# Two factors of a state-space input table turned once, kept in DRAM and multiplied per batch on VectorE

## The chip, the cores and the metric

One core of a Trainium2 chip runs the whole kernel; the other cores are idle. The metric is the device time of one execution in microseconds (us). The engines have these names in the profile: PE (TensorE, matmuls; PEld is its weight load), DVE (VectorE), ACT (ScalarE), POOL (GpSimd) and SP (SyncE, which here issues all the transfers, in its own order).

## The reference, cut to what matters

Two layers work on x of 1024 frames by 1024 channels. Layer 0 projects RMSNorm(x) into a state-space branch, a retention branch and their gates; layer 1 is a convolution module. The change concerns the state-space branch: 64 groups of 16 channels, each group with 64 complex states.

```python
dt  = exp(log_dt)
lb  = exp((a_re + 1j * a_im) * dt)              # one complex factor per group and state
bb  = (lb - 1) / a * (b_re + 1j * b_im)         # group x state x channel of the group
bu  = einsum('tgh,gnh->tgn', u, bb)             # input, 16 channels -> 64 states
x_t = lb * x_(t-1) + bu_t                       # scan over the frames
y   = Re(einsum('tgn,ghn->tgh', x, c)) + d * u
y   = gelu(y); y = y * sigmoid(y @ glu_w + glu_b)
y   = y * silu(gate)
```

The real and imaginary parts are float32 arrays of their own.

## The kernel before, in words

**Numbers.** The large matmuls split each float32 operand into a high and a low part and add three products (`mm3`, lines 137 to 144), all in one accumulation: 24 matmuls of 128x512 for one output tile of 128 channels by 512 frames. An output block `u0` to `u7` (state-space input) or `g8` to `g23` (gates) has two such tiles, 48 matmuls. A weight block is loaded from DRAM (`wload_pieces`, line 131), rounded to its high part on ACT (line 133), and the low part is formed by DVE or POOL (line 134); for the gate blocks that is DVE. Three buffers of each allow loads two blocks ahead. The matmul results go to three PSUM banks in turn (`mm`); DVE evicts a gate tile (line 325), ACT applies SiLU (line 326), SP stores it (line 329).

**The state-space branch in frames of 8.** The scan runs over blocks of 8 frames, so a state is carried 128 times, not 1024. For that each group needs tables: `M`, the input table (powers of `lb` for the 8 frames times `bb`); `Tc` and `Ts`, rotations that make the scan real; `W3`, the output table. `s5_params` forms the small factors for all groups on DVE and POOL: `pr`, `pi` (nine powers by 32 pairs of groups) and `bbr`, `bbi` (32 pairs by 16 channels), each with 128 partitions: two groups by 64 states.

**Batches.** The 64 groups are worked in 8 batches `B` of 8 groups (four pairs `q`). For each batch:
- `s5_tables(B)` has POOL form `M`, then `Tc` and `Ts`, then `W3`: 18 operations of 128x512 in a fixed chain over all batches. `Mr` and `Mi` have one buffer each; so the table of the next batch is written after `kp` of this batch has read it.
- `s5_states(B)`: SP loads the inputs `U` (line 678). PE turns `Mr` and `Mi` by four transposes each into PSUM (line 685) and ACT copies them to SBUF (line 687): this is `W2`, with 8 frames by 16 channels on the partitions and the states along the row. PE multiplies `W2` with `U` into `v` (line 696, 32 matmuls of 128 columns). DVE rotates (`m0`, `m1`), scans (line 711), rotates back (`d0`, `d1`) and writes the states `S`, of which there is one buffer (lines 704 to 724). PE forms the kernel of the short convolution, `kp`, from `Mr` and `Mi` (lines 730, 731) and turns it (`kt`, line 736); ACT copies it (`Kt`); SP stores it to DRAM (line 740) and loads it back skewed (`Wd`, line 743); ACT copies it to `W1` (line 745).
- `s5_out(B)`: PE forms `y` from `W1`, `U`, `W3`, `S` (lines 760, 766), ACT copies it (`yb`, line 770), SP stores it (line 772).

**Order of the work.** `layer0_front` runs two gate blocks per batch (lines 347 to 355): states of batch B, gate block, outputs of batch B - 1, gate block, tables of batch B + 1. A scheduler that plans with priorities in program order decides the final order on each engine; an engine then works strictly in that order and waits on semaphores. The gate matmuls fill PE between the small state-space products. The temporaries of the scan (`m0`, `m1`, `d0`, `d1`) share the four buffers of the tag `tmpV`; those of POOL have two of `tmpP`. The small products use five PSUM banks (`aux`).

After this stage come retention, the GLU and the output projection, and layer 1.

Of the kernel before, what the change touches and what calls it, by code (L numbers as in the profile page):

```python
# [11 lines left out]
F32 = mybir.dt.float32  # L12
# [3 lines left out]
ALU = mybir.AluOpType  # L16
# [3 lines left out]
P = 128  # L20
# [19 lines left out]
class Trunk:  # L40
# [163 lines left out]
    def layer0_front(self, st):  # L204
        tc, nc, A = self.tc, self.nc, self.A
# [30 lines left out]
        for kb in range(KB):  # L236
# [6 lines left out]
            t = xt[kb] = ev.tile([P, T], F32, name=f"x_{kb}", tag="xin", bufs=8)  # L243
            g = self.vec(V_NG0, kb)
            for h in range(2):
                c = slice(h * HALF, (h + 1) * HALF)
# [50 lines left out]
        def scaled(nb, w, name, cb):  # L297
            for h in range(2):
                ps = self.bank(f"mm_{name}_{h}", aux=False)
                self.gemm(ps[:], w, xs[h], {2: r_mm[h]} if nb == 2 else None)  # L300
                cb(h, ps)
# [18 lines left out]
        def gate_block(nb, w, dst):  # L320
            gt = uv.tile([P, T], F32, name=f"gt_{nb}", tag="ut", bufs=2)

            def evac(h, ps):
                c = slice(h * HALF, (h + 1) * HALF)
                nc.vector.tensor_tensor(gt[:, c], ps[:], self.R[:, c], op=ALU.mult)  # L325
                nc.scalar.activation(gt[:, c], gt[:, c], AF.Silu)
            scaled(nb, w, f"g{nb}", evac)
            k = nb % 8
            nc.sync.dma_start(dst[k * P:(k + 1) * P], gt[:])
# [17 lines left out]
        for nb in range(8, 24):  # L347
            B = (nb - 8) // 2
            if nb % 2 == 0:
                self.s5_states(B)  # L350
            gate_block(nb, self.wnext(f"g{nb}"), self.gs_d if nb < 16 else self.gr_d)
            if nb % 2 == 0 and B:
                self.s5_out(B - 1)
            if nb % 2 and B < 7:
                self.s5_tables(B + 1)
# [277 lines left out]
    def outer(self, B, o_r, o_i, ar, ai, br, bi, view, op_r=ALU.subtract, op_i=ALU.add):  # L633

        gp = self.nc.gpsimd
        for o, op, (a0, b0), (a1, b1) in ((o_r, op_r, (ar, br), (ai, bi)), (o_i, op_i, (ar, bi), (ai, br))):
# [2 lines left out]
            yield gp.tensor_tensor(view(o), a0, b0, op=ALU.mult)  # L639
            yield gp.tensor_tensor(o, o, t[:], op=op)  # L640

    def s5_tables(self, B):


        nc, w = self.nc, self.s5
        gp, v = nc.gpsimd, nc.vector
        qs = slice(4 * B, 4 * B + 4)

        Mr, Mi = self.big(f"Mr_{B}", "Mr", 1), self.big(f"Mi_{B}", "Mi", 1)
        vm = lambda ap: ap.rearrange("p q (j h) -> p q j h", j=8)  # L650
        bj = lambda t: t[:, qs, :].unsqueeze(2).broadcast_to([P, 4, 8, 16])
        pj = lambda t, o=0: t[:, o:o + 8, qs].rearrange("p j q -> p q j").unsqueeze(3).broadcast_to([P, 4, 8, 16])
        made = [self.outer(B, Mr[:], Mi[:], bj(self.bbr), bj(self.bbi), pj(self.pr), pj(self.pi), vm)]

        Tc, Ts = self.big(f"Tc_{B}", "Tc", 2), self.big(f"Ts_{B}", "Ts", 2)
        vt = lambda ap: ap.rearrange("p q (a b) -> p q a b", b=16)
        ea = lambda t: t[:, 0:8, qs].rearrange("p a q -> p q a").unsqueeze(3).broadcast_to([P, 4, 8, 16])
        eb = lambda t: t[:, 0:16, qs].rearrange("p b q -> p q b").unsqueeze(2).broadcast_to([P, 4, 8, 16])
        made.append(self.outer(B, Tc[:], Ts[:], ea(self.e2[0]), ea(self.e2[1]), eb(self.e1[0]), eb(self.e1[1]), vt))

        W3 = w.tile([P, 2, 4, P], F32, name=f"W3_{B}", tag="W3", bufs=2)
        made.append(self.outer(B, W3[:, 0], W3[:, 1], pj(self.pr, 1), pj(self.pi, 1), bj(self.cr), bj(self.nci), vm,
                               ALU.add, ALU.subtract))
        self.s5_last = self.chained(chain(*made), self.s5_last)
        R8 = self.big(f"R8_{B}", "R8", 2)
        for q in range(4):
            nc.scalar.mul(R8[:, q, :], self.m01[:], self.r8[:, 4 * B + q:4 * B + q + 1])
        self.s5_tab[B] = Mr, Mi, W3, Tc, Ts, R8

    def s5_states(self, B):  # L670
        nc, w = self.nc, self.s5
        gp, v = nc.gpsimd, nc.vector
        q0 = 4 * B
        Mr, Mi, W3, Tc, Ts, R8 = self.s5_tab.pop(B)


        U = w.tile([P, 8, P], F32, name=f"U_{B}", tag="U", bufs=2)
        nc.sync.dma_start(U[:], self.u_d[B].rearrange("j h g m -> (j h) g m"))


        W2 = []
        for nm, M in (("r", Mr), ("i", Mi)):
            ps = self.bank(f"w2{nm}_{B}")
            for q in range(4):
                nc.tensor.transpose(ps[:, q * P:(q + 1) * P], M[:, q, :], self.ident[:])
            t = self.big(f"W2{nm}_{B}", f"W2{nm}", 1)
            nc.scalar.copy(t[:].rearrange("p q n -> p (q n)"), ps[:])
            W2.append(t)

        V = []  # L690
        for c in range(2):
            ps = self.bank(f"v{c}_{B}")
            for q in range(4):
                for g2 in range(2):
                    r = slice(64 * g2, 64 * g2 + 64)
                    nc.tensor.matmul(ps[r, q * P:(q + 1) * P], W2[c][:, q, r], U[:, 2 * q + g2, :],
                                     start=True, stop=True)
            V.append(ps)
        fl = lambda t: t[:].rearrange("p q n -> p (q n)")

        tc, ts = fl(Tc), fl(Ts)
        vr, vi = V[0][:], V[1][:]
        t2, t4 = (fl(self.big(f"m{i}_{B}", "tmpV", 4)) for i in range(2))
        v.tensor_tensor(t2, vi, ts, op=ALU.mult)
        v.tensor_tensor(t4, vr, ts, op=ALU.mult)
        v.tensor_tensor(vr, vr, tc, op=ALU.mult)
        v.tensor_tensor(vi, vi, tc, op=ALU.mult)
        v.tensor_tensor(vr, vr, t2, op=ALU.add)
        v.tensor_tensor(vi, vi, t4, op=ALU.subtract)
        for z in (vr, vi):  # L710
            v.tensor_tensor_scan(z, fl(R8), z, 0.0, op0=ALU.mult, op1=ALU.add)

        S = w.tile([P, 2, 4, P], F32, name=f"S_{B}", tag="S", bufs=1)
        c1 = lambda t: t[:, :, 1:P]
        c0 = lambda t: t[:, :, 0:P - 1]
        zr, zi = (z.rearrange("p (q n) -> p q n", q=4) for z in (vr, vi))
        t2, t3 = (self.big(f"d{i}_{B}", "tmpV", 4) for i in range(2))
        v.tensor_tensor(c0(t2), c0(zi), c0(Ts), op=ALU.mult)
        v.tensor_tensor(c0(t3), c0(zr), c0(Ts), op=ALU.mult)
        v.tensor_tensor(c0(zr), c0(zr), c0(Tc), op=ALU.mult)  # L720
        v.tensor_tensor(c0(zi), c0(zi), c0(Tc), op=ALU.mult)
        v.tensor_tensor(c1(S[:, 0]), c0(zr), c0(t2), op=ALU.subtract)
        v.tensor_tensor(c1(S[:, 1]), c0(zi), c0(t3), op=ALU.add)
        v.memset(S[:].rearrange("p c q m -> p (c q) m")[:, :, 0:1], 0.0)


        kp = self.bank(f"kp_{B}")
        for q in range(4):
            o = kp[q * 32:(q + 1) * 32, :P]
            nc.tensor.matmul(o, self.cbr[:, q0 + q, :], Mr[:, q, :], start=True, stop=False)  # L730
            nc.tensor.matmul(o, self.cbni[:, q0 + q, :], Mi[:, q, :], start=False, stop=True)
        Kg = w.tile([P, P], F32, name=f"Kg_{B}", tag="Kg", bufs=1)
        nc.scalar.copy(Kg[:], kp[:, :P])
        v.tensor_tensor(Kg[:, :16], Kg[:, :16], self.dd[:, B, :], op=ALU.add)
        kp = self.bank(f"kt_{B}")
        nc.tensor.transpose(kp[:, :P], Kg[:], self.ident[:])
        Kt = w.tile([P, P], F32, name=f"Kt_{B}", tag="Kg", bufs=1)
        nc.scalar.copy(Kt[:], kp[:, :P])

        nc.sync.dma_start(self.k_d[B, 112:], Kt[:])  # L740
        Wd = w.tile([P, 8, P], F32, name=f"Wd_{B}", tag="yb", bufs=1)
        kd = self.k_d[B]
        nc.sync.dma_start(Wd[:], bass.AP(tensor=kd.tensor, offset=kd.offset, ap=[[P, P], [16 * P, 8], [1, P]]))
        W1 = w.tile([P, 8, P], F32, name=f"W1_{B}", tag="W1", bufs=2)
        nc.scalar.copy(W1[:].rearrange("p g (i h) -> p i g h", i=8), Wd[:].rearrange("p i (g h) -> p i g h", g=8))
        self.s5_back[B] = U, W1, W3, S
# [693 lines left out]
```

## Time and profile before

| what | value |
|---|---|
| time, median of 3 runs | 1219.36 us (1218.27 to 1221.7) |
| time of the profiled execution | 1219.24 us |
| its span, first to last instruction | 1217.5 us |
| mean granted clock of PE | 0.997 |
| `u` and start of the stage, first transposes of batch 0 | 101.20 us |
| `v` of batches 1 to 7 | 132.69, 162.21, 191.72, 221.23, 250.75, 280.26, 309.77 us |
| last `y` of the stage | 335.17 to 337.15 us |
| DVE, POOL busy in 150 to 200 us | 24.68 of 50, 38.61 of 50 us |
| DMA share in 100 to 300 us, per 50 us | 0.31, 0.35, 0.42, 0.35 |

How to read it: the span is cut by engine, line and tile names; a busy time is that of the instructions on one engine. The chain of waits follows the program back from its last instruction, at each step to what released it. Where an engine isn't on that chain, its idle time costs nothing by itself.

### The profile page before, as it was taken

To read this page: it belongs to the slowest core of one execution; us is meant where nothing else is said; L and a number is where in the kernel's file an instruction comes from. 1 tells how busy PE (TensorE), PEld (TensorE's weight loads), DVE (VectorE), ACT (ScalarE), POOL (GpSimd) and SP (SyncE) were. 2 spreads that over 40 slices of the span, in tenths; PEclk is the share of its full clock that TensorE was granted. 3 is DMA by queue.
4 is the path that set the end of the run, shared out by engine and by line. 5 is a ranking of instruction groups with operands and counts; after the bars stand their busy time and mean duration, and the time that the engine had idled before them with its cause. 6 is when DMAs were issued, how large, how long until landed. Compare 5 with 4: busy or idle time off the path is not lost.

```text
span 1217.5 us, 17581 instructions
## 1 busy us (share of the span) xinstructions
PE 1199.5 (99%) x6660; PEld 1011.3 (83%) x6660; DVE 747.1 (61%) x1337; ACT 480.6 (39%) x712; POOL 653.9 (54%) x453
## 2 busy tenths in 40 slices
PE   9999999999999999998999999999999999999997
PEld 7888888888889999997888888788888888888876
DVE  7965555555413635546746101599999799999533
ACT  7212233322222323134434322545545575434652
POOL 2059988888124333342454551578453467758642
PEclk9999999999999999999999999999999999999998
DMA  8342433333384536266446776755677654356764
GB/s 333 104 139 74 152 128 124 133 131 124 107 268 139 176 102 195 82 216 220 165 156 216 269 270 254 260 188 196 222 253 251 232 182 155 123 176 236 243 250 147
DMA packets 98500, 225.03 MB, mean 185 GB/s; under 512 B 9072, under 2 KB 38000, under 8 KB 97776
## 3 DMA queue, kind: packets, MB, share of 16 engines
q1 hardware_dynamic: 98416, 223.92, 54.9%
q8 instruction: 52, 0.85, 0.3%
q14 instruction: 32, 0.26, 0.1%
HBM read 158.41 MB, written 61.28 MB: 180 GB/s over the span
## 4 chain that ended last, share of the span: by engine, by line
PE 91%; DMA 4%; DVE 2%; ACT 1%; POOL 1%; issue 1%; SPq 1%; DVEq 0%; POOLq 0%
PE mm_g L143 7%; PE mm_g L144 7%; PE mm_g L142 7%; PE mm_wo L144 5%; PE mm_wo L142 5%; PE mm_wo L143 5%; PE mm_a L144 2%; PE mm_b L144 2%; PE mm_a L143 2%; PE mm_a L142 2%; PE mm_b L143 2%; PE mm_u L144 2%; PE mm_u L143 2%; PE mm_b L142 2%; PE mm_u L142 2%; PE mm_glu L144 2%
## 5 line engine op out<-in xcount | busy, mean ns | idle before, releaser
L1142 DVE SCALAR_TENSOR_TENSOR cv<-u,convw,cv 128x512 f32<-128x512 f32 x398 | 273.4, 751 | 11.9 <-ACT cv L1128 9.6
L1122 POOL TENSOR_TENSOR tp<-tp,tp 128x512 f32<-128x512 f32 x64 | 83.1, 1298 | 44.4 <-ACT tp L1121 43.3
L144 PE MATMUL mm_g<-xh,wl_g 128*128 128x512 f32 x256 | 100.8, 394 | 0.0
L143 PE MATMUL mm_g<-xl,wh_g 128*128 128x512 f32 x256 | 100.6, 393 | 0.0
L142 PE MATMUL mm_g<-xh,wh_g 128*128 128x512 f32 x256 | 100.5, 393 | 0.0
L861 PE MATMUL mm_v<-wh_v,xl 128*128 128x256 f32 x256 | 72.5, 283 | 0.0
L860 PE MATMUL mm_v<-wl_v,xh 128*128 128x256 f32 x256 | 72.4, 283 | 0.0
L859 PE MATMUL mm_v<-wh_v,xh 128*128 128x256 f32 x256 | 72.4, 283 | 0.0
L134 POOL TENSOR_TENSOR wl_v<-wf_v,wh_v 128x1024 fp32r<-128x1024 f32 x8 | 19.2, 2396 | 88.6 <-ACT wh_v L133 88.6
L1121 ACT ACTIVATE tp<-u,convw 128x512 f32<-128x512 f32 x64 | 45.7, 719 | 34.9 <-POOL tp L1122 33.2
L325 DVE TENSOR_TENSOR gt<-mm_g,R 128x512 f32<-128x512 f32 x32 | 21.9, 685 | 59.9 <-PE mm_g L144 59.9
L143 PEld LDWEIGHTS mm_g<-xl,wh_g 128*128 128x128 f32 x256 | 48.1, 188 | 11.3 <-issue 1.6
L144 PEld LDWEIGHTS mm_g<-xh,wl_g 128*128 128x128 f32 x256 | 48.0, 188 | 10.6
L142 PEld LDWEIGHTS mm_g<-xh,wh_g 128*128 128x128 f32 x256 | 48.1, 188 | 9.6
L144 PE MATMUL mm_oc<-zh,wl_woc 128*128 128x512 f32 (+1 forms) x152 | 54.0, 359 | 1.5 <-DMA wl_woc<-lo_woc 1.5
L1044 DVE TENSOR_TENSOR x<-mm_wo,xr 128x512 f32<-128x512 f32 x16 | 11.1, 692 | 71.9 <-PE mm_wo L144 51.4
L142 PE MATMUL mm_oc<-zh,wh_woc 128*128 128x512 f32 (+1 forms) x152 | 54.3, 363 | 0.0
L143 PE MATMUL mm_oc<-zl,wh_woc 128*128 128x512 f32 (+1 forms) x152 | 53.8, 357 | 0.5 <-POOL zl L969 0.5
L143 PE MATMUL mm_glu<-yl,wh_glu 128*128 128x512 f32 x128 | 50.3, 393 | 2.5 <-DVE yl L969 2.5
L144 PE MATMUL mm_wo<-yrh,wl_wor 128*128 128x512 f32 x128 | 50.0, 391 | 1.4 <-DMA wl_wor<-lo_wor 1.4
L143 PE MATMUL mm_u<-xl,wh_u 128*128 128x512 f32 x128 | 50.1, 391 | 0.8 <-DVE xl L257 0.7
L142 PE MATMUL mm_glu<-yh,wh_glu 128*128 128x512 f32 x128 | 50.1, 393 | 0.6 <-ACT yh L968 0.6
(393 smaller groups left out, 3600.7 us busy)
## 6 DMA issues: line engine op xcount, KB each, us to landing
wf_g<-w_ab SPq DMA_DIRECT2D x16, 512.0 KB, 4.0
wf_wos<-w_out SPq DMA_DIRECT2D x16, 512.0 KB, 5.0
wf_wor<-w_out SPq DMA_DIRECT2D x16, 512.0 KB, 5.8
wf_cb<-w_c SPq DMA_DIRECT2D x16, 512.0 KB, 4.4
wf_ca<-w_c SPq DMA_DIRECT2D x16, 512.0 KB, 4.7
wf_woc<-w_out_c SPq DMA_DIRECT2D x16, 512.0 KB, 5.0
wf_cg<-w_c SPq DMA_DIRECT2D x11, 512.0 KB, 4.4
u_d<-ut SPq DMA_DIRECT2D x8, 512.0 KB, 3.2
```

Source lines behind the costliest of these rows:

```text
L134: lo[i].tensor_tensor(wl[:].rearrange(fl)[:, c], wf[:, c], h.bitcast(F32), op=ALU.subtract)
L142: nc.tensor.matmul(ps, wh[:, kb, :], xh, start=start, stop=False)
L143: nc.tensor.matmul(ps, wh[:, kb, :], xl, start=False, stop=False)
L144: self.last_mm = nc.tensor.matmul(ps, wl[:, kb, :], xh, start=False, stop=stop)
L325: nc.vector.tensor_tensor(gt[:, c], ps[:], self.R[:, c], op=ALU.mult)
L859: nc.tensor.matmul(ps[:, :256], xh[:, o:o + P], wh, start=kb == 0, stop=False)
L860: nc.tensor.matmul(ps[:, :256], xh[:, o:o + P], wl, start=False, stop=False)
L861: nc.tensor.matmul(ps[:, :256], xl[:, o:o + P], wh, start=False, stop=kb == KB - 1)
L1044: v.tensor_tensor(t[:], ps[:], xt[:], op=ALU.add)
L1121: nc.scalar.mul(sk[:], u[:, k:k + HALF], cw[:, nb, k:k + 1])
L1122: gp.tensor_tensor(s0[:], s0[:], sk[:], op=ALU.add)
L1142: v.scalar_tensor_tensor(dst[:], *tap, accs_[i][:], op0=ALU.mult, op1=ALU.add)
```

## The change

After the states of batch 0, `s5_turned` is called once. It copies `bbr` and `bbi` into an order by channel (ACT), turns them and the first eight powers `pr`, `pi` with twelve transposes on PE, copies the three results to SBUF (ACT), and stores them to two DRAM tensors: `pt_d` (a row for each frame of 8 and pair of groups, 128 states long) and `bt_d` (a row for each of 16 channels and pair).

For each batch from 1 on, `s5_tables` now ends with `s5_w2(B)`. SP loads four tables of 128x512: `PTr` and `PTi` repeat a row of powers for the 16 channels, `BTr` and `BTi` repeat a row of `bb` for the 8 frames, so that partition (frame, channel) has both factors beside each other. Six DVE operations multiply them as complex numbers into `W2r` and `W2i`. The states of that batch use these; the transposes of line 685 and the copies of line 687 are left for batch 0 alone. POOL still forms `M` for all batches, since `kp` reads it.

The four loaded tables, the two reordered copies and the three turned ones all use the tag `tmpV`, with its four buffers as before. The order of the loads on the SP queue and of the six products on DVE is the scheduler's. In the built program it is, for batches 4 to 7 on SP: `PTr`, `BTr`, `k_d` of the batch before, `Wd`, a gate store, `U` (before or behind the gate store), a weight block, `PTi`, the store of `yb`, `BTi`. For batches 2 and 3 `BTi` is issued ahead of the store of `yb`. On DVE the first product (`W2r`) stands behind the rotations of the batch before, the other five behind its `S`, with the gate evictions between them.

```diff
@@ layer0_front
             if nb % 2 == 0:
                 self.s5_states(B)
+                if B == 0:
+                    self.s5_turned()
@@
+    def s5_turned(self):
+        nc = self.nc
+        self.pt_d = self.dram.tile([2, 2, P, P], F32, name="pt_d")
+        self.bt_d = self.dram.tile([2, 4, P, P], F32, name="bt_d")
+        fl = lambda t, a, n: t[:, a * n:(a + 1) * n, :].rearrange("p a b -> p (a b)")
+        order = [self.big(f"hq{c}", "tmpV", 4) for c in range(2)]
+        for o, t in zip(order, (self.bbr, self.bbi)):
+            nc.scalar.copy(o[:].rearrange("p a (h q) -> p (a h) q", h=4), t[:].rearrange("p q h -> p h q"))
+        for i, (dst, parts) in enumerate((
+                (self.pt_d[:].rearrange("c a r n -> r (c a) n"), [fl(t, a, 4) for t in (self.pr, self.pi) for a in range(2)]),
+                (self.bt_d[0].rearrange("a r n -> r a n"), [order[0][:, a, :] for a in range(4)]),
+                (self.bt_d[1].rearrange("a r n -> r a n"), [order[1][:, a, :] for a in range(4)]))):
+            ps = self.bank(f"turn{i}")
+            for a, src in enumerate(parts):
+                nc.tensor.transpose(ps[:, a * P:(a + 1) * P], src, self.ident[:])
+            t = self.big(f"turned{i}", "tmpV", 4)
+            nc.scalar.copy(t[:].rearrange("p q n -> p (q n)"), ps[:])
+            nc.sync.dma_start(dst, t[:])
+
+    def s5_w2(self, B):
+        nc, v = self.nc, self.nc.vector
+        (ptr, pti), (btr, bti) = ([self.big(f"{n}{c}_{B}", "tmpV", 4) for c in "ri"] for n in ("PT", "BT"))
+        dp, db = self.pt_d, self.bt_d
+        for c, (pt, bt) in enumerate(((ptr, btr), (pti, bti))):
+            nc.sync.dma_start(pt[:].rearrange("p q n -> p (q n)"),
+                              bass.AP(tensor=dp.tensor, offset=dp.offset + (c * 2 * P + 4 * B) * P,
+                                      ap=[[32 * P, 8], [0, 16], [1, 4 * P]]))
+            nc.sync.dma_start(bt[:].rearrange("p q n -> p (q n)"), bass.AP(tensor=db.tensor, offset=db.offset + (c * 4 * P + 4 * B) * P,
+                                                ap=[[0, 8], [32 * P, 16], [1, 4 * P]]))
+        w2r, w2i = (self.big(f"W2{nm}_{B}", f"W2{nm}", 1) for nm in "ri")
+        v.tensor_tensor(w2r[:], ptr[:], btr[:], op=ALU.mult)
+        v.tensor_tensor(w2i[:], ptr[:], bti[:], op=ALU.mult)
+        v.tensor_tensor(ptr[:], pti[:], bti[:], op=ALU.mult)
+        v.tensor_tensor(pti[:], pti[:], btr[:], op=ALU.mult)
+        v.tensor_tensor(w2r[:], w2r[:], ptr[:], op=ALU.subtract)
+        v.tensor_tensor(w2i[:], w2i[:], pti[:], op=ALU.add)
+        return [w2r, w2i]
@@ s5_tables
-        self.s5_tab[B] = Mr, Mi, W3, Tc, Ts, R8
+        self.s5_tab[B] = Mr, Mi, W3, Tc, Ts, R8, self.s5_w2(B) if B else None
@@ s5_states
-        Mr, Mi, W3, Tc, Ts, R8 = self.s5_tab.pop(B)
+        Mr, Mi, W3, Tc, Ts, R8, W2 = self.s5_tab.pop(B)
...
-        W2 = []
-        for nm, M in (("r", Mr), ("i", Mi)):
+        first, W2 = W2 is None, W2 or []
+        for nm, M in (("r", Mr), ("i", Mi)) if first else ():
             ps = self.bank(f"w2{nm}_{B}")
```

## The prediction

> **What bounds the kernel now.** I read the page's busy table and slices first, then the waits of TensorE (PE), then the chain of waits over the state-space stage (about 101 to 337 us), and last the timelines of the other engines there.
>
> ```profile
> PE 1199.5 (99%) x6660; PEld 1011.3 (83%) x6660; DVE 747.1 (61%) x1337; ACT 480.6 (39%) x712; POOL 653.9 (54%) x453
> ...
> POOL 2059988888124333342454551578453467758642
> PEclk9999999999999999999999999999999999999998
> ```
>
> PE is busy for 99% of the span at full granted clock; POOL (GpSimd) is nearly full in slices 4 to 10, the stage of this change. The waits of PE over the whole span begin with 2.5 us for `yl`, and none belongs to the state-space products. The chain in order of time shows the stage as a stretch of PE work alone (start, length, what):
>
> ```profile
> 244.84 0.44 PE w2r L685 x4
> 245.27 0.44 PE w2i L685 x4
> ...
> 250.75 1.90 PE v L696 x32
> ```
>
> So here every microsecond of PE work taken out shortens the kernel, and every wait put on PE lengthens it. One batch of eight takes 29.51 us (`v` at 221.23 and at 250.75), in which PE does 96 gate matmuls, one each 0.227 us.
>
> **What is removed and added on PE.** Batches 1 to 7 lose eight transposes: 0.44 + 0.43 us on the path, 0.87 each, 6.1 us in all. The one-time turn adds twelve of the same form, 12 x 0.109 = 1.3 us. Net -4.8 us, if PE never waits. The fourteen ACT copies that go (0.58 us each) and the five that come are off the path: ACT is 39% busy.
>
> **What is added on DVE (VectorE).** Six products per batch, each 128x512 float32 with both inputs in SBUF. The trace has that form: `yl` alone takes 0.68. Beside a busy POOL it doesn't (first row DVE, then POOL; then the same again):
>
> ```profile
> 366.07 2.88 DVE L836 TENSOR_TENSOR krot<-kraw,kswp 128x512 f32<-128x512 f32 x1 [1.20 <-POOL kswp L835]
> ...
> 366.00 2.40 POOL L134 TENSOR_TENSOR wl_k<-wf_k,wh_k 128x1024 fp32r<-128x1024 f32 x1
> ...
> 548.17 3.48 DVE L969 TENSOR_TENSOR yl<-yf,yh 128x512 fp32r<-128x512 f32 x2
> ...
> 549.37 1.74 POOL L1016 TENSOR_TENSOR yg<-yg,yn 128x512 f32<-128x512 f32 x1
> ```
>
> `krot` ends only 0.5 us after the POOL operation beside it. Two `yl` in a row take 3.48, 1.74 each, and POOL's own 1.29 becomes 1.74: the two engines take turns, a whole operation at a time. In the stage POOL issues table operations of 1.1 to 1.4 us back to back, so I price a product at 0.68 (free) to 1.74 (in turns), near 1.7 while POOL is busy, 0.6 for one that starts on an idle POOL.
> [...]
>
> Six times 1.7 is 10 us per batch on an engine with some 14 free of 29.5, so DVE doesn't become the bound; the question is when the last product is ready. `v` of the next batch must wait for it, and behind `v` on PE lies everything else. POOL's operations stretch by 0.45 per product, some 2.7 us per batch, of the 4 to 5 us that it idles for `kp`: no cost.
>
> **What sets the time of the last product.** The four loads per batch go into the four `tmpV` buffers that the scan of the batch before (`m0`, `m1`, `d0`, `d1`) holds; two wait until `S` is formed. In the built program's order on the SP queue, for batches 4 to 7, the last (`BTi`) is also behind the store of `yb`, which waits for the copies of `yb`, which on ACT come after the copy of `W1`, which waits for the load of `Wd`. Before, that chain read:
>
> ```profile
> 262.36 0.32 SPq L740 DMA_DIRECT2D k_d<-Kt  x1
> ...
> 263.92 0.37 SPq L743 DMA_DIRECT2D Wd<-k_d  x1
> ...
> 271.74 0.32 SPq L772 DMA_DIRECT2D y_d<-yb  x1
> ...
> 269.56 1.05 ACT L745 COPY W<-Wd 128x1024 f32<-128x1024 f32 x1 [5.86 <-DMA Wd<-k_d]
> 270.64 1.07 ACT L770 COPY yb<-y 128x512 f32<-128x512 f32 x2
> ```
>
> The store is issued 21.0 us after `v` (250.75). The new order puts the copy of `Kt` ahead of a weight cast (1.03), so I take 20.2. `BTi` follows at 20.6. It is 256 KB in rows of 2 KB, like these:
>
> ```profile
> yg<-gs_d SPq DMA_DIRECT2D x16, 256.0 KB, 3.2
> yn<-yn_d SPq DMA_DIRECT2D x16, 256.0 KB, 2.8
> ```
>
> With the store's 512 KB just ahead (2.6 us) I take 3.8: landed at 24.4. No row shows sixteen partitions reading one DRAM row; the bounds are 2.8 and the 8.4 us of `s_s_br` (256 KB behind a full queue).
>
> From 24.4 DVE does a product (25.5), the gate's eviction (26.1), and the next two in turns with POOL (27.2, 28.9). POOL started 2.6 after `v`, has 24.2 us of work (223.85 to 248.08) and four stretches, so it ends near 28.6; the subtraction then ends at 29.5 if POOL has finished, 30.6 if not: 30.05. Unhindered, PE reaches the next `v` after 94 matmuls here, 94 x 0.227 + 2.49 (`v`, `kp`) + 3.78 (`y`) + 0.11 = 27.7, or 96 and 28.2. So a batch waits 2.4 or 1.9 us. What queues behind: on SP the gate's store and the next weight load (20 us early); on DVE the next gate evictions, with three PSUM banks of 5.45 us each as cover.
>
> By the same steps:
> - Batch 1: turn, store to DRAM, load back. `turned2` waits on ACT behind two gate copies; store about 125, last load lands about 132, last product about 139, against `v` at 138.1 (126.78 + 44 x 0.227 + 1.3): 1.0 us, 0 to 3.
> - Batch 2: its `v` comes only 77 matmuls after batch 1's, 23.85 us; `BTr` lands at 14.6, so `S` and `BTi` are late (20.2), and the products meet a full POOL: 26.4, and the second part another 1.1 late. 3.7 us, 1.5 to 5.
> - Batch 3: `BTi` goes ahead of the store of `yb`: lands at 19, ready 25.1 against 25.2; the second part 0.7 late.
> - Batch 4: 2.4. Batches 5 and 6: 1.9 each. Batch 7: 0.5, since `Kt` needn't wait for the copies of `R8` (1.3).
>
> Together 12.1 us of new waits.
>
> **The sum.** -6.1 + 1.3 + 12.1 = +7.3. The profiled execution took 1219.24 (span 1217.5 and 1.7 around it), 0.1 below the median shown, 1219.36; the forecast is 1226.5. One microsecond either way in the landing of `BTi` moves five batches, 5 us, and the turns on POOL two or three more: its own range is 1220 to 1235.
>
> [...]
>
> **Rivals.**
> - *The products are ready in time.* If loads land in 2.8 us and products cost 0.68, batch 5 has `BTi` at 23.4 and the subtraction at 26.5, before 28.2; batch 2, with BTi at 19.8, at 22.9, before 23.85. Then only -4.8 is left: 1214.4. For it: `yl` at 0.68 and DVE's free time. Against it: 1.74 beside POOL.
> - *Waits and savings cancel.* Landings 1.0 us earlier and POOL done sooner: waits of 4 to 6 us: 1219.
> - *The loads are the slow part (slower, far).* Many partitions read one DRAM row, with 1 MB more per batch in a stage that moves 100 to 150 GB/s. From a landing over 5 us this decides: at 8.4, 4.6 later, six batches lose 28 us more: 1254. For it: `Wd`, an overlapping read too, takes 5.2 for 512 KB. Against it: that isn't above its like; the DMA share is 0.31 to 0.42.
> - *DVE becomes the bound of the stage (slower).* 15 us of DVE work now (24.7 to 29.3 per 50 us) and 10 of products stay under 28.6 us per batch. It decides from a product of 2.3 us on; at `krot`'s 2.88 a batch takes 15 + 17.3 = 32.3, so 2.8 more than 29.51, times 7, plus 1.3: 1240. Against it: no operation of POOL in the stage is as long as the 2.40 beside `krot`, but when DVE stretches it.
>
> **How the numbers follow.** Forecast (1220 to 1235) 0.55, in time 0.15, cancel 0.15, slow loads 0.07, DVE bound 0.08. 0.3% is 3.7 us, about what a measurement of this kernel can tell from no change. Below 1215.7: the first rival, 0.15. Within: the second, and the lower edge of the forecast, 0.20 together. Above 1223: 0.65. The range 1214 to 1240 leaves out half of the first rival and of the bound by DVE, and the slow loads: 0.19.
>
> **What would show it.** PE's waits: `v` for the last subtraction or addition, 0.5 to 4 us in most batches; the period of `v` near 30 us for batches 4 to 6 rather than 28.6. DVE: products of 1.2 to 1.8 while POOL is busy, 0.68 after. SP: `BTi` issued right behind the store of `yb`, landing in 3 to 5 us. `w2r` and `w2i` four transposes each, batch 0 alone. I am wrong if PE waits for nothing in the stage, if the loads take 2.5 or 8 us, or if the wait ends on POOL or a weight load.

## The result, and the profile after

The changed kernel takes 1235.47 us (median of 6 runs, 1232.12 to 1238.74) against 1219.26 of the kernel before in the same series: a ratio of 1.013, 95% interval 1.0112 to 1.0147, or some 16 us more. The profiled execution took 1235.18 us, its span is 1233.4. Line numbers of the changed kernel are higher by 43 behind the new functions: `v` is L739, the products are L677 to L682, the loads L671 (`PT`) and L674 (`BT`).

The page of the changed kernel, its busy table and slices:

```profile
PE 1201.5 (97%) x6616; PEld 1012.3 (82%) x6616; DVE 788.3 (64%) x1379; ACT 478.0 (39%) x703; POOL 652.1 (53%) x453
...
PE   9999888999999999999999999999999999999997
...
POOL 2069577787414152433354552388463368767642
PEclk9999889999999999999999999999999999999999
```

PE lost 44 instructions, as the change says, and yet is busy 2.0 us longer. The eighths stand in slices 5 to 7 (123 to 216 us), in PE's own row and in two slices of the granted clock: all that was lost lies in the state-space stage. POOL is no longer full there. PE's waits in the stage (line, what it waited for: us in all, times, longest):

```profile
PE v L739 <- issue: 7.5, 2, 4.2
PE v L739 <- DVE W2r L681: 3.7, 1, 3.7
PE v L739 <- ACT wh_g L133: 1.7, 2, 0.9
PE v L739 <- DVE W2i L682: 1.7, 1, 1.7
PE v L739 <- ACT wh_k L133: 0.5, 1, 0.5
```

There were none before; now there are 15.2 us, every one on `v`. "issue" stands where the profile shows nothing that the engine waited for. Where "issue" or ACT's cast `wh_g` is named, the cast had long been done, and DVE's subtraction for `W2r` had ended just ahead of `v`.

The chain in order of time (start, length, what), from the turn to the `v` of batch 2:

```profile
121.49 4.46 DMA pt_d<-turned
...
127.33 5.72 DMA bt_d<-turned
133.06 5.57 DMA BTi<-bt_d
138.66 0.70 DVE W2i L678
...
141.46 3.68 PE v L739 x32
...
168.29 4.24 issue
172.52 3.65 PE v L739 x31
```

Where there was only PE before, there is now a store, a load, products, and a `v` that takes 3.68 us where it took 1.90. The windows around the first wait say why (stretch, its length, then busy time with instructions of PE, PEld, DVE, ACT, POOL, then the granted clock, DMA share and GB/s):

```profile
137.80:139.60 1.80, 0.00 (x1) 0.00 (x0) 0.91 (x2) 0.00 (x0) 0.00 (x0) 1.00 0.81 245
139.70:141.40 1.70, 0.00 (x0) 0.00 (x0) 1.67 (x4) 0.00 (x0) 0.00 (x0) 0.58 0.48 195
141.40:146.80 5.40, 5.34 (x50) 4.54 (x51) 2.77 (x6) 0.89 (x2) 0.51 (x1) 0.50 0.00 1
146.80:150.00 3.20, 3.20 (x16) 2.61 (x15) 3.20 (x6) 1.60 (x2) 3.12 (x4) 1.00 0.02 5
```

The granted clock falls to 0.50 within the second stretch, some 2 us into the wait, and stays there through the third, for 5.3 us of PE's work.

The SP queue ahead of the last load for batch 5, and DVE behind it:

```profile
246.81 0.38 SPq L786 DMA_DIRECT2D Wd<-k_d  x1
249.16 0.32 SPq L329 DMA_DIRECT2D gr_d<-gt  x1
249.53 0.42 SPq L721 DMA_DIRECT2D U<-u_d  x1
250.23 0.49 SPq L131 DMA_DIRECT2D wf_g<-w_ab  x1
250.82 0.60 SPq L671 DMA_DIRECT2D PTi<-pt_d  x1
252.24 0.31 SPq L815 DMA_DIRECT2D y_d<-yb  x1
252.65 0.60 SPq L674 DMA_DIRECT2D BTi<-bt_d  x1
```

```profile
259.61 0.80 DVE L678 TENSOR_TENSOR W2i<-PTr,BTi 128x512 f32<-128x512 f32 x1 [8.20 <-DMA BTi<-bt_d]
...
261.96 0.69 DVE L680 TENSOR_TENSOR PTi<-PTi,BTr 128x512 f32<-128x512 f32 x1
262.57 0.68 DVE L681 TENSOR_TENSOR W2r<-W2r,PTr 128x512 f32<-128x512 f32 x1
```

`BTi` is issued 18.1 us after `v` (234.54) and is 6.96 us on its way, with 2.75 MB issued in the six microseconds ahead of it; DVE stands idle for it for 8.2 us. The last products then run at 0.68 to 0.69. One of these waits has another cause: the 1.7 us before the second half of batch 7's `v` come from the last addition, which stood beside a POOL operation of 2.45 us (`wl_k`, line 134):

```profile
322.00 2.84 DVE L682 TENSOR_TENSOR W2i<-W2i,PTi 128x512 f32<-128x512 f32 x1
```

From the start of the first `v` to the end of the last `y`, the stage went from 230.1 to 247.6 us. PE's work there at full clock is 230.1 - 6.1 + 1.3 = 225.3; its waits are 15.2, and it was busy 232.4, so 7.1 more than its work: that is the lowered clock. What lies ahead of the stage and behind it took 1.6 us less (0.33 and 1.24). The sum is +15.9 of span.

### The profile page after: what moved, and what is told of

Read it like the earlier page. It is cut to its first block, busy times and chain, and to the rows that moved or that the text cites. A ratio compares the mean times of both kernels' runs of the same rounds, so it can differ in the third digit from the quotient of the medians.

```text
span 1233.4 us, 17582 instructions
## 1 busy us (share of the span) xinstructions
PE 1201.5 (97%) x6616; PEld 1012.3 (82%) x6616; DVE 788.3 (64%) x1379; ACT 478.0 (39%) x703; POOL 652.1 (53%) x453
## 4 chain that ended last, share of the span: by engine, by line
PE 82%; DMA 7%; DVE 5%; issue 3%; ACT 2%; POOL 1%; SPq 1%; DVEq 0%; POOLq 0%
PE mm_g L144 5%; PE mm_g L143 5%; PE mm_g L142 5%; PE mm_wo L144 5%; PE mm_wo L143 5%; PE mm_wo L142 5%; PE mm_b L143 2%; PE mm_b L144 2%; PE mm_a L143 2%; PE mm_a L144 2%; PE mm_b L142 2%; PE mm_a L142 2%; PE mm_u L144 2%; PE mm_u L143 2%; PE mm_u L142 2%
## 5 line engine op out<-in xcount | busy, mean ns | idle before, releaser
L326 ACT ACTIVATE gt<-gt 128x512 f32<-128x512 f32 x32 | 20.2, 632 | 112.8 <-DVE gt L325 100.8
```

## The experiments

All are compared with the kernel before on the same chip (its medians there: 1219.3 to 1220.6). Stage: from the first `v` to the end of the last `y` in the profiled run. Clock: PE's busy time there less its work at full clock (230.1 and what was removed and added). Waits: the rest of the stage. Behind: the span from there on, whose work is the same in all.

| kernel | median, us | ratio, 95% | stage | clock | waits | behind |
|---|---|---|---|---|---|---|
| before | 1219.26 | 1 | 230.1 | 0.0 | 0.0 | 880.3 |
| changed | 1235.47 | 1.0112 to 1.0147 | 247.6 | 7.1 | 15.2 | 879.1 |
| e1 own buffers | 1232.16 | 1.0072 to 1.0104 | 242.1 | 4.1 | 12.7 | 881.1 |
| e2 own, from batch 2 | 1221.24 | 0.9986 to 1.0009 | 233.3 | 2.4 | 4.7 | 879.1 |
| e3 turn alone | 1220.97 | 0.9995 to 1.0014 | 231.5 | 0.1 | 0.0 | 881.2 |
| e4 rows apart | 1223.94 | 1.0011 to 1.0038 | 233.2 | 2.2 | 5.8 | 879.0 |
| e5 rows apart, same tensor | 1227.35 | 1.0038 to 1.0088 | 237.4 | 2.4 | 9.7 | 879.4 |
| e6 from batch 4 | 1231.50 | 1.0071 to 1.0111 | 238.4 | 3.7 | 6.8 | 883.9 |
| e7 28 transposes | 1234.95 | 1.0103 to 1.0145 | 247.8 | 3.4 | 9.4 | 878.3 |
| e8 own, from batch 3 | 1224.09 | 1.0017 to 1.0042 | 230.1 | 0.3 | 2.8 | 883.3 |
| e9 own, from 2, Kg first | 1216.07 | 0.9967 to 0.9984 | 227.0 | 0.1 | 0.7 | 880.7 |
| e10 e9, rows apart | 1216.08 | 0.9961 to 0.998 | 226.2 | 0.0 | 0.0 | 880.7 |
| e11 PT apart | 1229.11 | 1.0068 to 1.0101 | 244.0 | 4.6 | 14.1 | 880.8 |
| e12 BT apart | 1230.14 | 1.0069 to 1.0095 | 238.0 | 2.6 | 10.1 | 880.6 |
| e13 28 matmuls | 1241.34 | 1.0169 to 1.0204 | 249.3 | 0.2 | 4.6 | 882.2 |
| e14 14 matmuls | 1237.91 | 1.0107 to 1.0159 | 247.1 | 3.4 | 8.5 | 880.7 |
| e15 19, 23, 8 matmuls | 1237.40 | 1.011 to 1.0163 | 243.1 | 0.2 | 5.9 | 887.4 |

**e1: buffers of their own.**

```diff
-        t2, t4 = (fl(self.big(f"m{i}_{B}", "tmpV", 4)) for i in range(2))
+        t2, t4 = (fl(self.big(f"m{i}_{B}", "tmpV", 2)) for i in range(2))
...
-        (ptr, pti), (btr, bti) = ([self.big(f"{n}{c}_{B}", "tmpV", 4) for c in "ri"] for n in ("PT", "BT"))
+        (ptr, pti), (btr, bti) = ([self.big(f"{n}{c}_{B}", "tmpT", 4) for c in "ri"] for n in ("PT", "BT"))
```

> The turned tables and the two ordered copies get four buffers of their own, the scan's temporaries keep two, R8 one (for the room), so the four loads of a batch no longer wait for the scan of the batch before, and BTi is no longer issued behind the stores of yb. Theory (a loop from v through the scan, its buffers, the late loads and the products to the next v): from batch 3 on PE waits for no product, the half clock behind the waits goes, about 15.1 us of waits and 5.6 us of clock shrink to those of batch 1 and perhaps 2 (4 and 3 us): 1216 to 1222. Rival 1 (the products themselves are too dear on DVE beside POOL): the waits stay, over 1228. Rival 2 (a load with repeated rows is slow whenever it runs): the loads are still 5 us and more, but early, so this one tells nothing against the theory by its time; the landing does.

Measured 1232.16, ten more than the theory gave. Its waits in the stage:

```profile
PE v L739 <- DMA U<-u_d: 9.1, 2, 7.5
PE v L739 <- issue: 3.6, 1, 3.6
```

The second line is batch 1. The first is a wait that no theory had named: the loads of the next batch now start early and stand on SP in front of the load of `U`, which is late for batches 2 and 3. For batch 2 `BTr` is issued only at 162.28, when the product that frees its buffer is done; `Wd` and `U` stand behind it, so that `U` goes out at 163.47, 0.9 us before PE stops for it. From batch 4 on, though, the theory holds: no wait at all, `v` every 28.65 us (29.51 - 0.87), and this although products beside a busy POOL take up to 1.91, as those for batch 6:

```profile
271.30 1.91 DVE L681 TENSOR_TENSOR W2r<-W2r,PTr 128x512 f32<-128x512 f32 x1
...
276.11 1.48 DVE L682 TENSOR_TENSOR W2i<-W2i,PTi 128x512 f32<-128x512 f32 x1
```

```profile
288.39 1.09 PE L739 MATMUL v<-U,W2r 128*64 128x128 f32 x16
```

They end 10 us ahead of that `v`, which has no bracket for a wait. So dear products alone (rival 1) don't make the waits.

**e2: the same, from batch 2 on.**

```diff
-        self.s5_tab[B] = Mr, Mi, W3, Tc, Ts, R8, self.s5_w2(B) if B else None
+        self.s5_tab[B] = Mr, Mi, W3, Tc, Ts, R8, self.s5_w2(B) if B > 1 else None
```

> As e1, and batch 1 goes by transposes like batch 0, so that the first turned tables are wanted a batch later. Removed 6 x 0.87 = 5.2, added 1.3, so -3.9 if nothing waits. Theory: no wait of PE on v over 0.5 us, clock near 0.997, 1215.3 (1214 to 1218), faster than the kernel before by some 0.3%. Rival 1 (products too dear beside POOL): over 1225. Rival 3 (what was lost is batch 1's own chain of turn, store and load alone, and the later batches only follow from it): this one shows it too, and is told apart by the run with shared buffers from batch 2 on.

Measured 1221.24: 11 us better than e1, not faster than before. No `v` waits. One other wait is left:

```profile
PE kt L779 <- DVE Kg L777: 4.7, 1, 4.7
```

It is batch 2's, and the clock falls within it. On DVE the first two products of batch 3 (1.59 and 1.86) stood in front of the addition for `Kg`.

**e3: the turn alone.** The last item of `s5_tab` is `None` for all batches.

> The factors are turned and stored as in the changed kernel, but every batch makes its W2 by transposes, as before. Theory: twelve transposes more, 1.3 us, and three stores beside other loads: 1220.5 (1219.5 to 1222). Rival (the turn itself is dear: its copies on ACT, its stores on the SP queue, its buffers of the scan's): 3 us or more, over 1222.5.

1220.97; the stage is 1.4 us longer, PE never waits. The theory holds: the turn costs its 1.3 us.

**e4 and e5: the rows of the loads.** e4 reads another input, e5 the stored factors. This is e5's edit, with the old load of `bt` left out:

```diff
-            nc.sync.dma_start(pt[:].rearrange("p q n -> p (q n)"),
-                              bass.AP(tensor=dp.tensor, offset=dp.offset + (c * 2 * P + 4 * B) * P,
-                                      ap=[[32 * P, 8], [0, 16], [1, 4 * P]]))
...
+            for t in (pt, bt):
+                nc.sync.dma_start(t[:].rearrange("p q n -> p (q n)"),
+                                  bass.AP(tensor=db.tensor, offset=db.offset + c * 4 * P * P, ap=[[4 * P, P], [1, 4 * P]]))
```

> As the changed kernel, but the four loads of a batch read 128 separate rows of 2 KB of another input instead of 8 or 16 rows for all partitions; this leaves out that W2 is the product of the turned factors (its values are others). Theory (BTi is slow for what stands in the queues ahead of it): issue to start of the product stays 5.6 to 8.5 us, time 1233 to 1238. Rival 2 (sixteen partitions that read one row are slow): the load falls to about 3 us, by 2.5 to 5 us in six batches, time 1215 to 1225. Batch 1 gains in both, since its load no longer waits for the store of the turned factors: up to 3.7 us less by the theory too, 1230.

> As the changed kernel, each load of a batch behind the same stores and from the same DRAM tensor (bt_d, for the PT loads too), but with 128 separate rows of 2 KB instead of 8 or 16 rows for all partitions; this leaves out that W2 is made of the right factors. Against e4 it keeps batch 1's store in front of its load. Theory 1 (BTi lands late only for what is queued ahead of it): landings of 5.6 to 8.5 us as in the changed kernel, 1233 to 1238. Theory 2 (a row that is read by 8 or 16 partitions costs some 2.4 us a load, the difference of the medians 7.0 and 4.6 between the changed kernel and e4): BTi in 3 to 6.6 us, waits of batches 2 to 7 as in e4 (5.2 us in all), batch 1 some 2.5 us better than the changed kernel's 3.7: 1224 to 1228.

e4 came to 1223.94 and e5 to 1227.35, both in the range of slow rows (rival 2 of e4, theory 2 of e5); theory 1, a queue and nothing else, falls. From issue to the product that waits for it, `BTi` took 5.6, 5.1, 8.6, 5.7, 7.0, 7.0, 8.5 us in the changed kernel (median 7.0) and 5.0, 3.7, 5.2, 4.9, 5.7, 4.0, 7.1 in e5 (5.0). In the chain of e5, batch 4's load, 5.65 us in the changed kernel:

```profile
217.08 4.90 DMA BTi<-bt_d
```

Of the 3.4 us between e4 and e5, batch 1, whose load in e4 had no store to wait for, is 1.9: its `v` starts at 139.09 without a wait in e4, at 140.98 after 1.91 in e5. Another 1.6 is a wait for `W2i` in batch 7.

The traces also show how such a load is slow. Here only the loads of `PTr` and `BTr` for one batch are under way, first in the changed kernel, then in e5 (columns as in the windows above; the last two are the busy share of the 16 DMA engines and GB/s):

```profile
242.00:243.50 1.50, 1.50 (x8) 1.20 (x7) 1.50 (x3) 0.63 (x1) 1.50 (x2) 1.00 0.48 184
...
263.00:264.00 1.00, 1.00 (x6) 0.84 (x5) 1.00 (x2) 0.00 (x0) 1.00 (x1) 1.00 1.00 379
```

The loads with repeated rows keep the DMA engines half as busy (0.48 against 1.00) and move at half the rate (184 against 379 GB/s). As an estimate from these rows, 256 KB take 1.42 us instead of 0.69; with 0.27 us more for the issue on SP (0.60 in the rows for batch 5, 0.33 in e4), `PTi` and `BTi` together lose 2.0 us, the difference of the medians. Both patterns of the changed kernel begin with a dimension of 8 (`[32 * P, 8]` and `[0, 8]`), those of e4 and e5 with one of 128; no run tells whether that or the repetition of rows halves the rate.

**e11 and e12: one pair of loads each.**

> As the changed kernel, with only the two PT loads reading 128 separate rows (of bt_d; so the left factors are others); the two BT loads read 16 rows, each for 8 partitions that lie 16 apart. In e5, with all four apart, the time was 8.1 us under the changed kernel's 1235.5. If the PT loads (8 rows, each for 16 neighbouring partitions) are the slow ones: 1227 to 1229. If both alike: 1231. If the BT loads: 1234 to 1236.

> The other half of e11: only the two BT loads read separate rows (the right factors are others), the PT loads read 8 rows, each for 16 neighbouring partitions. If the PT loads are the slow ones: 1234 to 1236. If both alike: 1231. If the BT loads: 1227 to 1229.

1229.11 and 1230.14: both alike, within the runs' scatter (e11's profiled run, 1234.58, was the slowest of its four; batch 1 waited 5.42 us in it). Eight rows for 16 neighbouring partitions each and 16 rows for 8 distant ones cost about the same. The gains don't add: 6.4 and 5.3 us here, 8.1 together in e5.

**e6: from batch 4 on, shared buffers.** As e2's edit, with `B > 3`, on the changed kernel.

> As the changed kernel, but the turned tables serve batches 4 to 7 alone; 1 to 3 go by transposes. Removed 4 x 0.87 = 3.5, added 1.3: -2.2 without waits. Theory (the late loads cost each batch what they cost batches 4 to 7 of the changed kernel, 0.9 + 0 + 0.8 + 2.2 = 4.0, none long enough for the half clock; the rest of the loss is batches 1 to 3): +1.8, 1222 (1220 to 1224). Rival a (the waits of batches 4 to 7 are only left over from the three before): no waits, 1218.2. Rival b (the wait of the first batch that goes this way is always long, whichever it is): a wait of over 3 us before batch 4, half clock behind it, 1225 or more.

1231.50: rival b, the first batch pays, whichever it is. `v` of batch 4 waited 2.65, then 1.0, 0.9, 0.6 and 1.7 came for the others, 6.8 in all where 4.0 were expected. The rival's wait of over 3 us wasn't needed: 2.65 us sufficed for the clock, and the clock fell once more, at 315.36, behind batch 7's wait of 1.7 us. The windows around the first fall:

```profile
219.60:222.10 2.50, 0.00 (x0) 0.00 (x0) 2.46 (x4) 0.00 (x0) 0.60 (x1) 1.00 0.00 0
222.20:223.20 1.00, 1.00 (x19) 1.00 (x21) 1.00 (x3) 0.00 (x0) 0.00 (x0) 1.00 0.08 16
223.20:226.60 3.40, 3.40 (x36) 2.59 (x33) 2.78 (x5) 0.90 (x2) 0.52 (x1) 0.50 0.52 173
```

Of the 3.6 us behind the stage, 2.6 are longer waits of PE and 1.0 is PE's busy time, with one fall of the clock there (at 578 us); what made those waits is open.

**e7, e13, e14, e15: is it the clock?** Work put on PE ahead of `v` of batches 1 to 3, to be overwritten; it depends on nothing, and its place in PE's order is tied to the subtraction for `W2r`:

```diff
+            for q in range(28 if c == 0 and B in (1, 2, 3) else 0):
+                self.chained([nc.tensor.transpose(ps[:, q % 4 * P:q % 4 * P + P], self.ident[:], self.ident[:])], self.warm)
```

> As the changed kernel, with 28 transposes of the identity (28 x 0.109 = 3.05 us, their result is overwritten) put on PE ahead of v in batches 1 to 3, so that PE works through most of the 3.3 to 4.2 us that it waited there; they displace 6 to 12 gate matmuls to behind v. Theory (the half clock is granted because PE stood still for over 3 us): v takes 1.9 us in all batches, granted clock 0.997, up to 5.6 us less than the changed kernel: 1230 (1228 to 1232), though 3 x 3.05 us of work are added. Rival (the clock falls for another reason, or its effect is hidden in the wait for the next products): 1235 to 1244.

> As e7, with 28 full matmuls (identity by identity, overwritten) in place of the 28 transposes ahead of v in batches 1 to 3; a full 128x128 matmul takes about the same, 0.112 us each by the y rows, 3.1 us in all. In e7 the granted clock still fell to 0.50 behind batches 1 and 2, after waits of 2.1 and 3.1 us that followed 3.1 us of transposes, and the time was the changed kernel's. Theory A (transposes don't count as work for the clock, matmuls do; and the half clock delays the chain that leads to the next v): no fall of the clock, or one shorter, each of the three batches up to 1.8 us sooner: 1230 to 1233. Theory B (the next v's time is set by the loads, which wait for other things; what PE loses at half clock it would have waited): clock full, time as before, 1234 to 1237. Theory C (any wait of over 2.5 us lowers the clock, whatever ran before it): clock 0.50 behind batch 2 as in e7.

> As e13 with 14 matmuls instead of 28: e13's took 0.229 us each, 6.4 us a batch, more than the waits that they were to fill, so that v came later by itself. 14 take 3.2 us, as long as e7's transposes. Theory A (the half clock delays the chain that leads to the next v): clock 1.00 behind all three batches, each v up to 1.8 us sooner than the one before it allows in the changed kernel, 1230 to 1233. Theory B (what PE loses at half clock it would have waited): clock 1.00 and 1234 to 1237, with waits of PE on v longer than in e7 (9.4 us) by what is no longer lost to the clock. Theory C (a wait of over 2.5 us lowers the clock, whatever ran before it): 0.50 behind batch 2.

> As e14, with 19, 23 and 8 matmuls ahead of v in batches 1, 2 and 3 (4.4, 5.3 and 1.8 us), so that less than 1 us of each wait is left and nothing overshoots. In e13, with the clock at 1.00 throughout, W2r of the next batch was ready 28.9 and 28.7 us after v of batches 1 and 2; in the changed kernel, at half clock, 31.0 and 31.2. Theory A (the half clock delays the chain that leads to the next v): clock 1.00 behind all three, v of batch 3 some 4 us sooner after that of batch 1 than the changed kernel's 62.3 us, 1230 to 1233. Theory B (what PE loses at half clock it would have waited): 62 us again, 1234 to 1237.

e7 missed: the clock still fell behind batches 1 and 2, and the time was the changed kernel's. Putting matmuls in place of the transposes (e14, of the same length) changed nothing in that, so it isn't shown that e7 failed because its work was transposes. e13's filler was too long (0.229 us a matmul, not 0.112) but its clock stayed up. In e15 it did so without an overshoot, and `v` of batch 3 came 58.5 us after that of batch 1, not 62.3 as in the changed kernel, and not 61.9 as in e14, whose filler stood in the same place but whose clock fell: theory A's mechanism, the half clock delays the chain to the next `v`. The stage is 4.5 us shorter than the changed kernel's although 11.6 us of filler were added. Theory A's time (1230 to 1233) missed: 1237.40, with 887.4 us behind the stage in the profiled run (1240.02, the slowest of its four), 8.4 more than the changed kernel's. PE was busy 5.4 us longer there, with three falls of the clock (at 574, 591 and 697 us) where the changed kernel has none before its last microseconds, and it waited 2.9 longer. So the clock's share is shown in the stage, not in the time of the whole.

**e8: own buffers, from batch 3 on.**

> As e2 (own buffers for the turned tables), but from batch 3 on. Removed 5 x 0.87 = 4.4, added 1.3: -3.1. Theory: in e2 batches 4 to 7 ran at 28.65 us each without a wait, and only batch 2's kt waited 4.7 us for Kg behind products on DVE; here nothing waits: 1217.4 (1216 to 1219). Rival (a wait for Kg, pushed back on DVE by the products, comes with the first batch, whichever it is): 4.7 us and some clock more, 1221 to 1224.

1224.09: the rival, with a smaller wait. `kt` waited 1.9 us for `Kg`, one `v` 0.9, so that the stage came out level with before; 3.0 us came behind it.

**e9 and e10: Kg ahead of the products.**

```diff
-        v.tensor_tensor(w2r[:], ptr[:], btr[:], op=ALU.mult)
+        self.chained([v.tensor_tensor(w2r[:], ptr[:], btr[:], op=ALU.mult)], self.s5_kg)
...
-        v.tensor_tensor(Kg[:, :16], Kg[:, :16], self.dd[:, B, :], op=ALU.add)
+        self.s5_kg = v.tensor_tensor(Kg[:, :16], Kg[:, :16], self.dd[:, B, :], op=ALU.add)
```

The same for the product into `w2i`; everything else as e2. `chained` orders two instructions without a wait on a semaphore.

> As e2 (own buffers, from batch 2 on), with the first two products of a batch placed behind the addition of Kg on DVE. Removed 6 x 0.87 = 5.2, added 1.3: -3.9. In e2 PE waited 4.7 us for Kg in batch 2, and between the first v and the last y it was busy 2.3 us longer than its work takes at full clock. Theory (DVE's queue, with a product in front of Kg, made that wait): the wait falls by the product's 1.6 us or more, to 3 us or less, and with it the lowered clock; 1215.4 if nothing is left of it, 1218.5 if 3 us are. Rival (Kg is late on ACT, behind the copy of W1 that waits for the load of Wd): the wait stays over 4 us, 1221.

> As e9, with the four loads reading 128 separate rows of bt_d (as in e5; the factors are then not those of the right rows). Theory (a load of repeated rows costs time on the path only where it is late; here it is early): the products wait for nothing in either, as e9 within 1.5 us. Rival (the repeated rows hold up what stands behind them, the load of Wd among it, and so Kg): 2 to 5 us less than e9.

1216.07, faster than the kernel before by 0.16 to 0.33%. DVE's order in batch 2:

```profile
163.91 1.01 DVE L777 TENSOR_TENSOR Kg<-Kg,s_s_dd 128x16 f32<-128x16 f32 x1
164.85 0.68 DVE L677 TENSOR_TENSOR W2r<-PTr,BTr 128x512 f32<-128x512 f32 x1
```

and the stage (first `v` to the end of the last `y`):

```profile
107.40:334.30 226.90, 226.24 (x1544) 188.92 (x1543) 167.25 (x208) 65.99 (x120) 186.00 (x130) 1.00 0.47 156
```

Over the whole stage PE is busy 226.3 us, 3.8 less than the 230.1 of before; 6 x 0.87 - 1.3 is 3.9. e10 is level with e9 (1216.08 and 1216.07): a slow load with repeated rows costs nothing where it is early.

## Why the prediction was wrong

The direction was right, and so was the mechanism: PE waits on `v` for products whose last load is late. The size was not: +7.3 forecast, 16 measured. Two terms of the sum failed, and they hang together: the way of `BTi` was put at 3.8 us and took 7.0 (median), and the sum held nothing for the lowered clock, which took 7.1 us. In the profiled runs the 8.6 us between +7.3 and +15.9 are 3.1 of longer waits (15.2, not 12.1) and 7.1 of clock, less 1.6 outside the stage. The steps:

- *PE's own work, -4.8:* right. e3 shows the turn at 1.4, e9 the saving within 0.1, and batches that wait for nothing run 0.87 shorter.
- *Products at about 1.7 beside POOL, some 10 us per batch:* too dear. Beside a busy POOL a product took 0.68 to 1.91 in e1, e2 and e9, and the six of a late batch together 6.3 (e1) to 8.5 us (e9). In the changed kernel the last load came so late that POOL had mostly finished, and four of six products ran near 0.7. Beside an idle POOL the rows show 0.68 to 0.69 (batch 1 of the changed kernel). DVE had 41 us more work, not 70.
- *"With the store's 512 KB just ahead (2.6 us) I take 3.8: landed at 24.4":* this is the first step that failed. `BTi` took 5.1 to 8.6 us. The bounds, 2.8 and 8.4, held five of the seven; the value was taken from the end with like shapes (`yg`, `yn`), whose rows are all different. Of the 3.2 us by which the median of 7.0 exceeds it, 2.0 go with separate rows (e5), and with them 8.1 of the 16 us of time: the rate of such a load is half that of separate rows, 184 against 379 GB/s. The other 1.2 stay in e5; that they are the queue, 2.75 MB ahead rather than 512 KB, is argued, not shown.
- *The waits one by one, 12.1 in all:* 15.2 measured, but elsewhere. Batches 4 to 7 were put at 6.7 and waited 4.1, of which 1.7 is the addition beside POOL in batch 7 (the DVE rival had counted on no operation of POOL as long as 2.40 in the stage; `wl_k` took 2.45): `BTi` was issued 17.5 to 18.3 us after `v` in batches 5 to 7, not 20.6, and products were cheaper, which offset the landing. Batches 1 to 3 were put at 1.0, 3.7 and 0.7 and waited 3.7, 4.2 and 3.3. For batch 1 PE reached `v` at 137.8, as forecast (138.1), but the stores took 4.5 and 5.7 us in the chain and the load behind them 5.6, so that it landed at 138.7, not at 132. For batch 3 `BTi` landed 27.7 us after `v`, not 19: it was issued at 19.1 and took 8.6.
- *The clock:* the second step that failed. The sum had nothing for it. With three waits over 3 us (3.7, 4.2 and 3.3) where one was forecast (3.7) it was 7.1 us of PE's time. The granted clock of 0.997 in the profile before is a mean, and it hides a fall to 0.50 at 1210.73 us that lasts to the end, behind a wait of 1.2 us among the last small matmuls. This term follows from the last one, and e15 shows that it also lengthens the chain to the next `v`, by some 2 us each time.
- *The rivals:* products in time (1214.4) is near what e9 shows once the loads are early (1216.07, from batch 2 on). Slow loads priced each microsecond of landing in full (1254 at 8.4); measured, less reached the end, because the issue came sooner. DVE never became the bound.
- *What would show it:* PE's waits on `v` for the last subtraction came, and the period near 30 for batches 4 to 6 (30.75, 28.8, 29.6); "I am wrong if the loads take 2.5 or 8 us" came true in batches 3 and 7.

What stays open: which property of its pattern halves the rate of a load; and what makes PE's waits in the stretch behind the stage, which with the same work took from 878 to 887 us in these profiles (PE busy 864 to 869 us of it).

## What to carry to other kernels

A load that replaces work on a full engine is worth what it promises only if its buffers are free a whole period ahead: ask what frees the buffer, what stands in front of the load in its queue, and what the load in turn stands in front of (`U` in e1, `Kg` in e2). Price a load by a row of the same access pattern, and where there is none, take the dear end. And count small waits by their length, not by their sum: here one wait of 4.7 us (e2) went with 2.4 us of lowered clock, and 4.6 us in five waits of up to 1.7 (e13) with 0.2.

## What the runs showed of the hardware

- In the state-space stage the granted clock fell to 0.50 behind every wait of PE of 2.86 us (e5) or more, 13 in all. Below that, length alone doesn't decide: it fell behind 2.65 and 1.71 (both e6), 2.09 (e7) and 1.95 us (e14), the last two behind 3.2 to 3.3 us of identity transposes or matmuls, but not behind 2.42 (e12) and 2.32 (e5):

```profile
195.30:197.60 2.30, 0.00 (x0) 0.00 (x0) 2.27 (x4) 0.00 (x0) 1.09 (x1) 1.00 0.00 0
197.60:202.00 4.40, 4.36 (x56) 3.72 (x57) 4.40 (x7) 0.90 (x2) 1.59 (x2) 1.00 0.40 130
```

  It stayed down for 6.8 us in the six falls that came while PE still waited (so behind the first two waits of the changed kernel, from 140.0 to 146.8 and from 170.7 to 177.5 us) and for 3.4 us in the eleven that came after the wait had ended (from 204.8 to 208.2 us in the changed kernel, from 223.2 to 226.6 in e6).
- A load of 256 KB whose pattern begins with 8 steps, with rows read by 8 or 16 partitions each, moved with a DMA share of 0.48 at 184 GB/s (a pair of loads alone in the changed kernel), against 1.00 and 379 GB/s with 128 separate rows (e5). On the path it took 2 us longer (medians 7.0 and 5.0), and its issue on SP 0.60 us instead of 0.33 (e4).
- A product of 128x512 on DVE with both inputs in SBUF took 0.68 to 0.69 us beside an idle POOL, up to 1.91 beside POOL's table operations (e1), and 2.84 beside the 2.45 us of `wl_k` (the changed kernel, batch 7).
